# Down projection of the gated MLP: a part's first product one tile sooner, the third copy into SBUF, the next strip's sums later, one buffer apart for the summed pieces

## Chip, core and metric

One core of one Trainium2 chip runs the whole program in one launch. The metric is the time of an execution on the device in microseconds (us), as a median over runs. The profile is one further execution with the hardware profiler on.

## What is computed

Two residual layers on a 512 x 1024 activation (SEQ 512, D_MODEL 1024), each a token mixer and a gated MLP with d_ff = 2816. The mixers (gated linear attention in layer 0, softmax attention in layer 1) are not touched. The part that matters is the MLP:

```
def conv_ffn(h, w_up, w_conv, b_conv, w_down):
    u = h @ w_up
    u = lax.conv_general_dilated(
        u, w_conv[:, None, :], window_strides=(1,), padding=[(1, 1)],
        dimension_numbers=('NWC', 'WIO', 'NWC'), feature_group_count=u.shape[-1]) + b_conv
    val, gate = jnp.split(u, 2, axis=-1)
    return (jax.nn.silu(gate) * val) @ w_down
...
    for i in range(DEPTH):
...
        x = x + conv_ffn(rmsnorm(x, norm_ffn[i]), ffn_w_up[i], ffn_w_conv[i],
                         ffn_b_conv[i], ffn_w_down[i])
```

## The kernel before

**Numbers in two pieces.** Every float32 operand of a matmul is held as a high piece (fp32r) and a low piece, the rest. One product is then three matmuls: high by high, high by low, low by high.

**Tiles of the MLP.** The hidden width 2816 is 22 strips of 128 columns; strip m has a value half and a gate half. For each m, `act_up` (L656) makes two tiles of 128 x 512 in PSUM, t = 0 in a bank with the tag "acc" and t = 1 in a bank "s". Each takes 8 x 3 = 24 matmuls of 512 columns (L332 to L334). Behind them DVE scales (u, L672), ACT and DVE do the convolution (y: L674, L675, L676), ACT applies silu (L678), and DVE multiplies the two (L679). The activations of strips 2p and 2p+1 are then turned into the operands of the down product by `prepare` (L688): POOL and DVE form differences, and the helper `split` cuts each into two pieces on ACT (L685) and DVE (L686).

**Parts of the down product.** The first 16 strips are multiplied with the down weights by a scheme of Strassen's kind, in two parts of eight strips each, `down_part` (L712). By the table `DOWN_AFTER` = {9: 0, 17: 1}, part 0 stands behind strip m = 9 and part 1 behind m = 17, in both layers. A part has four strips n, and a strip has seven products of 12 matmuls each, 256 columns wide (all on L730; the tile that they write is called r). Their order in strip n: product 1 into r1 (`begin`), a copy r2 <- r1 on ACT (L739), product 6 onto r2, a copy r3 <- r2 (ACT, L747), 7 into r4, 2 onto r1, 5 onto r2, a third copy of r2 into the right half of r3's bank (ACT, L752), a DVE addition of r1 to x (L753), product 4 onto the left half of r3, product 1 of the next strip, two DVE subtractions of r4 and of the whole r3 from x (L758, L759), product 3 onto r2, and an addition of r2 to x (L761).

**Weights.** `Weights` loads a strip of 1 MB into one of two buffers "raw" (issued on SP, L129) and makes its pieces in the order of the list `todo`, some pieces ahead of their use. An up tile's piece is a copy on ACT (high, L190) and a subtraction on DVE (low, L191). A strip of the down weights has four pieces, h = 0 to 3 (`summed`, L144):

- h = 0 holds the operands of products 7 and 1: two sums on DVE (L150, L151, the second in place in raw), then high on ACT (L173) and low on DVE (L174).
- h = 1, for 5 and 6, is a sum on DVE (L155), then the same two lines.
- h = 2, for 2 and 4, has both copies on ACT (L169, L170); the low one is finished by an accumulating DMA that POOL issues (L180).
- h = 3, for 3, is half as wide (L162, L164, L165).

High pieces have tag "wh", low pieces "wl", four buffers each of 128 x 1024, shared by all weights.

**What orders the work.** The source is not the order on the engines: a scheduler in the compiler places each engine's instructions, and matmuls of one product can be set ahead of the rest of it. On each engine the result runs in order, and an instruction that waits holds up all behind it.

Of the kernel before, what the change touches and what calls it, by code (L numbers as in the profile page):

```python
# [8 lines left out]
F32 = mybir.dt.float32  # L9
F32R = mybir.dt.float32r  # L10
# [4 lines left out]
P = 128  # L15
S = 512
# [38 lines left out]
def hybrid_encoder_kernel(  # L55
# [39 lines left out]
    def pair(tag, bufs, dt, n):  # L95
        return sp.tile([P, 2 * S], dt, tag=tag, bufs=bufs, name=nm(n))
# [14 lines left out]
    class Weights:  # L111
# [2 lines left out]

        def __init__(self):
            self.todo, self.made, self.raw, self.by_dma, self.pending = [], {}, {}, [], []
            self.sums = {}

        def add(self, src, strips=None, pieces=2):
            for i in strips or range(src.shape[0]):  # L120
# [4 lines left out]
        def make(self, key):  # L125
            src, i, h = key
            if h == 0 and (id(src), i) not in self.raw:
                t = sp.tile([P, 4 * S], F32, tag="raw", bufs=2, name=nm("raw"))
                sync.dma_start(t, src[i])  # L129
                self.raw[id(src), i] = t  # L130
            if (id(src), i) in self.sums:
                self.made[id(src), i, h] = self.summed(self.raw[id(src), i], self.sums[id(src), i], h)
                return
            r = self.raw[id(src), i][:, h * 2 * S : (h + 1) * 2 * S]
            hi, lo = pair("wh", 4, F32R, "wh"), pair("wl", 4, F32R, "wl")
            if any(src is a and i < n for a, n in self.by_dma):
                act.activation(hi, r, AF.Copy)
                act.activation(lo, r, AF.Copy, scale=-1.0)  # L138
                self.pending.append((lo, r))
            else:  # L140
                self.split(hi, lo, r, 2 if src is w_vg and i < 2 else 1, src is w_vg and i == 0 and h == 0)
            self.made[id(src), i, h] = (hi, lo)

        def summed(self, raw, sums, h):  # L144


            a21, a11, a12, a22 = (raw[:, n * S : (n + 1) * S] for n in range(4))
            if h == 0:
                sums["e"] = e = big(F32, "sum")
                dve.tensor_tensor(e[:, :S], a21, a22, ALU.add)  # L150
                dve.tensor_tensor(a21, a21, a11, ALU.add)  # L151
                r = raw[:, : 2 * S]
            elif h == 1:
                e = sums["e"]
                dve.tensor_tensor(e[:, S:], e[:, :S], a11, ALU.add)  # L155
                r = e
            elif h == 2:
                r = raw[:, 2 * S :]
            else:
                e = sums["e"]  # L160
                r = tmp("sq", "sum4")
                dve.tensor_tensor(r, e[:, S:], a12, ALU.add)  # L162
                hi, lo = (sp.tile([P, S], F32R, tag="sq", bufs=3, name=nm(n)) for n in ("wh4", "wl4"))
                act.activation(hi, r, AF.Copy)  # L164
                dve.tensor_tensor(lo, r, hi.bitcast(F32), ALU.subtract)  # L165
                return hi, lo
            hi, lo = pair("wh", 4, F32R, "wh"), pair("wl", 4, F32R, "wl")
            if h == 2:
                act.activation(hi, r, AF.Copy)  # L169
                act.activation(lo, r, AF.Copy, scale=-1.0)  # L170
                self.pending.append((lo, r))
            else:
                act.activation(hi, r, AF.Copy)  # L173
                dve.tensor_tensor(lo, r, hi.bitcast(F32), ALU.subtract)  # L174
            return hi, lo
# [32 lines left out]

    W = Weights()
    up = [w_up[i] for i in range(2)]  # L210
    down = [w_down[i] for i in range(2)]

    def add_ffn(layer):
        first = 0
        for m, part in DOWN_AFTER.items():
            W.add(up[layer], range(first, m + 1))
            W.add(down[layer], range(part * NQ, (part + 1) * NQ), 4)
            first = m + 1
        W.add(up[layer], range(first, FC))
        W.add(down[layer], range(NPART * NQ, down[layer].shape[0]))  # L220

    for a in (w_vg, w_kq, w_gout):
        W.add(a)
# [185 lines left out]
    def gla(norm, nxt):  # L409
# [38 lines left out]

        rraw = sp.tile([P, KC * 32], F32, tag="sq", bufs=3, name="rraw")
        sync.dma_start(rraw, w_r)  # L450
        rw = pair("wh", 4, F32R, "rw")
# [198 lines left out]


    def ffn(layer, norm, cw, nxt):
        plain = {}
        quads = {}

        def act_up(m):  # L656

            res, pss = [], []
            for t in range(2):
                ps = bank("s" if t else "acc", "up")  # L660
                feature_tile(*W.half(up[layer], 2 * m + t, 3 if m in DOWN_AFTER and t else 1), norm.hl, ps)
                pss.append(ps)
                if m == 0 and t == 0:
                    norm.tokens()
                elif m == 0:
                    norm.rows()
            for t in range(2):
                ps = pss[t]
                cc = ((layer * 2 + t) * FC + m) * 4
                w = lambda i: cw[:, cc + i : cc + i + 1]  # L670
                u = tmp("u", "u")
                dve.tensor_tensor(u, ps, norm.R, ALU.mult)  # L672
                y = tmp("t", "y")
                act.activation(y, u, AF.Identity, scale=w(1), bias=w(3))  # L674
# [3 lines left out]
            act.activation(res[1], res[1], AF.Silu)  # L678
            dve.tensor_tensor(res[0], res[0], res[1], ALU.mult)  # L679
            return res[0]  # L680
# [28 lines left out]

        PLACE = {1: (0, S), 7: (0, 0), 6: (1, S), 5: (1, 0), 2: (2, 0), 4: (2, S), 3: (3, 0)}  # L710

        def down_part(part, then):  # L712

            src = down[layer]
            pairs = [quads.pop(part * NQ + i) for i in range(NQ)]
            st = [{} for _ in range(NQ)]
            pieces = {}

            def product(n, i, dst, start):
                h, o = PLACE[i]
                if (n, h) not in pieces:
                    pieces[n, h] = W.piece(src, part * NQ + n, h, 3)
                wh, wl = pieces[n, h]
                for j in range(NQ):
                    sl = slice(o + j * P, o + (j + 1) * P)
                    mh, ml = pairs[j][i]
                    for a, (w, m) in enumerate(((wh, mh), (wh, ml), (wl, mh))):
                        mm(dst, w[:, sl], m, start=start and j == 0 and a == 0, stop=j == NQ - 1 and a == 2,  # L730
                           skip_group_check=True)
                W.flush()

            def begin(n):
                r = st[n]
                r[1] = bank("acc", "r1")
                product(n, 1, r[1][:, :H], True)
                r[2] = bank("acc", "r2")
                act.activation(r[2][:, :H], r[1][:, :H], AF.Copy)  # L739

            begin(0)
            for n in range(NQ):
                r, c, d = st[n], x[2 * n], x[2 * n + 1]
                r1, r2 = r[1][:, :H], r[2][:, :H]
                product(n, 6, r2, False)
                r3 = bank("s", "r3")
                act.activation(r3[:, :H], r2, AF.Copy)  # L747
                r4 = bank("pt", "r4")
                product(n, 7, r4[:, :H], True)
                product(n, 2, r1, False)  # L750
                product(n, 5, r2, False)
                act.activation(r3[:, H:], r2, AF.Copy)  # L752
                dve.tensor_tensor(c[:, :H], c[:, :H], r1, ALU.add)  # L753
                product(n, 4, r3[:, :H], False)
# [3 lines left out]
                dve.tensor_tensor(two(d), two(d), two(r4[:, :H]).to_broadcast([P, 2, H]), ALU.subtract)  # L758
# [3 lines left out]
                if n == 1 and then is not None:  # L762
                    then()

        def end(c, ps):
            if nxt is not None or c < KC - 1:
# [10 lines left out]
        last = None  # L777
        for m in range(FC):
            y = act_up(m)
            if m >= 2 * NQ * NPART:  # L780
# [5 lines left out]
            elif m not in DOWN_AFTER:  # L786
                prepare(m // 2, last, y)
            if m in DOWN_AFTER:
                down_part(DOWN_AFTER[m], (lambda: prepare(m // 2, last, y)) if m < 2 * NQ * NPART else None)
        cur, open_ = None, {}  # L790
        for u, (c, k) in enumerate(PLAIN):
            if u % 8 == 0:
                cur = W.half(down[layer], NPART * NQ * 2 + u // 8)
# [313 lines left out]
```

## Time and profile before

| what | value |
|---|---|
| median of 3 runs | 1137.65 us (1137.04 to 1137.72) |
| the profiled execution, its own time | 1136.9 us |
| its span, from the first to the last instruction | 1135.2 us |
| PE (matmul) busy | 1119.9 us, 99% of the span |
| DVE, ACT, POOL busy | 793.1, 551.2, 121.4 us (70%, 49%, 11%) |
| matmuls of the down parts (L730), high and low | 164.5 and 125.5 us, 896 and 448 matmuls |
| PE waits put down to the copy on L739 | 5.7 us in 4 waits |

In the rows of the profile, L730 is a line of the kernel as it was before, an arrow reads "output <- inputs", and "[1.62 <-ACT r L739]" says that the engine was idle for 1.62 us ahead of this row and that the ACT instruction of L739 on tile r ended the wait. Matmuls overlap, so PE's busy time says less than the distance between the starts of two rows.

### The profile page before, as it was taken

To read this page: it belongs to the slowest core of one execution; us is meant where nothing else is said; L and a number is where in the kernel's file an instruction comes from. 1 tells how busy PE (TensorE), PEld (TensorE's weight loads), DVE (VectorE), ACT (ScalarE), POOL (GpSimd) and SP (SyncE) were. 2 spreads that over 40 slices of the span, in tenths; PEclk is the share of its full clock that TensorE was granted. 3 is DMA by queue.
4 is the path that set the end of the run, shared out by engine and by line. 5 is a ranking of instruction groups with operands and counts; after the bars stand their busy time and mean duration, and the time that the engine had idled before them with its cause. 6 is when DMAs were issued, how large, how long until landed. Compare 5 with 4: busy or idle time off the path is not lost.

```text
span 1135.2 us, 14636 instructions
## 1 busy us (share of the span) xinstructions
PE 1119.9 (99%) x5836; PEld 957.2 (84%) x5836; DVE 793.1 (70%) x1204; ACT 551.2 (49%) x818; POOL 121.4 (11%) x114
## 2 busy tenths in 40 slices
PE   9999999999999999999999999999999999999998
PEld 7788888888889988898888888888888998889887
DVE  6786653667888577776755679766788857777672
ACT  6565233444456444553464667544445644455340
POOL 0104110001011000000014333000100100000000
PEclk9999999999999999999999999999999999999999
DMA  6322210323225432253357633032322543225322
GB/s 234 144 97 89 75 46 29 111 75 111 74 75 133 164 111 96 73 133 146 130 125 173 157 103 75 1 112 74 111 75 75 132 165 112 89 79 132 147 74 75
DMA packets 22292, 120.16 MB, mean 106 GB/s; under 512 B 2640, under 2 KB 3280, under 8 KB 10704
## 3 DMA queue, kind: packets, MB, share of 16 engines
q1 hardware_dynamic: 17328, 102.29, 25.8%
q0 software_dynamic: 4608, 16.78, 7.8%
q8 instruction: 46, 0.75, 0.3%
q14 instruction: 22, 0.18, 0.0%
q10 hardware_dynamic: 288, 0.15, 0.0%
HBM read 100.34 MB, written 2.10 MB: 90 GB/s over the span
## 4 chain that ended last, share of the span: by engine, by line
PE 86%; DVE 6%; DMA 2%; issue 2%; ACT 2%; POOL 1%; SPq 0%; DVEq 0%; ACTq 0%; POOLq 0%
PE r L730 12%; PE up L333 12%; PE up L332 12%; PE up L334 11%; PE op L389 8%; PE vg L363 7%; PE dn L334 2%; PE dn L333 2%; PE dn L332 2%; PE o L614 2%; DMA wl<-raw 1%; PE pt L968 1%; PE av L363 1%; PE kv L590 1%; DMA raw<-in_w_down_dram 1%
## 5 line engine op out<-in xcount | busy, mean ns | idle before, releaser
L332 PE MATMUL up<-xhl,wh 128*128 128x512 f32 x704 | 274.3, 390 | 0.0
L333 PE MATMUL up<-xhl,wh 128*128 128x512 f32 x704 | 274.0, 389 | 0.0
L334 PE MATMUL up<-xhl,wl 128*128 128x512 f32 x704 | 273.9, 389 | 0.0
L190 ACT ACTIVATE wh<-raw 128x1024 fp32r<-128x1024 f32 x132 | 139.0, 1056 | 212.7 <-PE up L333 114.3
L191 DVE TENSOR_TENSOR wl<-raw,wh 128x1024 fp32r<-128x1024 f32 x132 | 163.8, 1241 | 52.4 <-ACT wh L190 52.4
L730 PE MATMUL r<-gu,wh 128*128 128x256 f32 x896 | 164.5, 285 | 7.1 <-ACT r L739 5.7
L332 PEld LDWEIGHTS up<-xhl,wh 128*128 128x128 f32 x704 | 132.2, 188 | 27.2
L333 PEld LDWEIGHTS up<-xhl,wh 128*128 128x128 f32 x704 | 132.2, 188 | 27.2
L334 PEld LDWEIGHTS up<-xhl,wl 128*128 128x128 f32 x704 | 132.1, 188 | 27.2
L730 PEld LDWEIGHTS r<-gu,wh 128*128 128x128 f32 x896 | 139.1, 191 | 11.8 <-ACT r L739 6.6
L730 PE MATMUL r<-gu,wl 128*128 128x256 f32 x448 | 125.5, 285 | 1.1 <-DVE wl L174 0.9
L672 DVE TENSOR_TENSOR u<-up,R 128x512 f32<-128x512 f32 x88 | 60.3, 687 | 45.0 <-PE up L334 45.0
L674 ACT ACTIVATE y<-u,cw 128x512 f32<-128x512 f32 x88 | 71.1, 811 | 35.5 <-DVE u L672 35.5
L730 PEld LDWEIGHTS r<-gu,wl 128*128 128x128 f32 x448 | 84.9, 191 | 2.3 <-DVE wl L174 1.3
L363 PE MATMUL vg<-wh,xhl 128*128 128x512 f32 x256 | 79.9, 391 | 0.3 <-DVE halfneg L250 0.3
L389 PE MATMUL op<-oT,wh 128*128 128x512 f32 x256 | 70.9, 395 | 0.0
L675 DVE SCALAR_TENSOR_TENSOR y<-u,cw,y 128x511 f32<-128x511 f32 x88 | 65.6, 747 | 4.2 <-ACT y L674 4.1
L676 DVE SCALAR_TENSOR_TENSOR y<-u,cw,y 128x511 f32<-128x511 f32 x88 | 65.8, 750 | 2.3
L678 ACT ACTIVATE y<-y 128x512 f32<-128x512 f32 x44 | 27.8, 632 | 71.8 <-DVE y L676 71.7
L180 POOL DMA_DIRECT2D wl<-raw x32 | 28.2, 881 | 303.6 <-ACT wl L138 140.4
L363 PEld LDWEIGHTS vg<-wh,xhl 128*128 128x128 f32 x256 | 47.9, 188 | 10.7 <-ACT sq L306 0.6
L389 PEld LDWEIGHTS op<-oT,wh 128*128 128x128 f32 x256 | 47.1, 188 | 9.7 <-ACT oT L629 0.3
(215 smaller groups left out, 1842.4 us busy)
## 6 DMA issues: line engine op xcount, KB each, us to landing
raw<-in_w_up_dram SPq DMA_DIRECT2D x44, 1024.0 KB, 4.8
raw<-in_w_down_dram SPq DMA_DIRECT2D x22, 1024.0 KB, 4.8
wl<-raw POOLq DMA_DIRECT2D x32, 512.0 KB, 4.6
raw<-in_w_vg_dram SPq DMA_DIRECT2D x6, 1024.0 KB, 4.8
raw<-in_w_akq_dram SPq DMA_DIRECT2D x5, 1024.0 KB, 4.8
raw<-in_w_kq_dram SPq DMA_DIRECT2D x4, 1024.0 KB, 4.8
raw<-in_w_gout_dram SPq DMA_DIRECT2D x4, 1024.0 KB, 4.8
raw<-in_w_aout_dram SPq DMA_DIRECT2D x4, 1024.0 KB, 4.8
```

What stands on the lines that cost most here:

```text
L190: act.activation(hi[:, sl], r[:, sl], AF.Copy)
L191: dve.tensor_tensor(lo[:, sl], r[:, sl], hi[:, sl].bitcast(F32), ALU.subtract)
L332: mm(ps, wh, mh, start=start, stop=False)
L333: mm(ps, wh, ml, start=False, stop=False)
L334: mm(ps, wl, mh, start=False, stop=stop)
L363: mm(ps[j][:, :width], hl[k][i == 2][:, j * P : (j + 1) * P], (wl if i == 1 else wh)[:, sl], start=k == 0 and i == 0, stop=k == KC - 1 and ...
L389: mm(pss[ng][n], wt[:, sl], mv, start=k == 0 and i == 0, stop=k == KC - 1 and i == 2)
L672: dve.tensor_tensor(u, ps, norm.R, ALU.mult)
L674: act.activation(y, u, AF.Identity, scale=w(1), bias=w(3))
L675: dve.scalar_tensor_tensor(y[:, 1:], u[:, : S - 1], w(0), y[:, 1:], ALU.mult, ALU.add)
L676: dve.scalar_tensor_tensor(y[:, : S - 1], u[:, 1:], w(2), y[:, : S - 1], ALU.mult, ALU.add)
L730: mm(dst, w[:, sl], m, start=start and j == 0 and a == 0, stop=j == NQ - 1 and a == 2, skip_group_check=True)
```

## The change

- **First product sooner.** `down_part` becomes a generator. For m = 9 and m = 17, `act_up` starts it between the two up tiles, so product 1 of strip 0 and the copy behind it are issued ahead of tile t = 1. The rest is run where the part stood. In `todo` the piece h = 0 of the part's first strip changes places with the piece of the up tile t = 1 of strip m. The call of `prepare` in the middle of the part takes its arguments from `late`.
- **Third copy.** It goes to an SBUF tile r5 of 128 x 256 (tag "u") and no longer to the right half of r3's bank. The subtraction of r3 (512 wide) becomes two of 256: one of r5, one of r3.
- **Sums later.** The two sums of h = 0 (L150, L151) are placed behind `self.last`, the low piece of h = 3 that was issued last, by `issue_after`.
- **Buffers.** "wh" and "wl" go from four buffers to three, and the pieces h = 1 get "sh" and "sl" with one buffer each. The space is the same.

```
+            self.sums, self.last = {}, None
...
-            hi, lo = pair("wh", 4, F32R, "wh"), pair("wl", 4, F32R, "wl")
+            hi, lo = pair("wh", 3, F32R, "wh"), pair("wl", 3, F32R, "wl")
...
-                dve.tensor_tensor(e[:, :S], a21, a22, ALU.add)
-                dve.tensor_tensor(a21, a21, a11, ALU.add)
+                with tc.issue_after(self.last.ins) if self.last else ExitStack():
+                    dve.tensor_tensor(e[:, :S], a21, a22, ALU.add)
+                    dve.tensor_tensor(a21, a21, a11, ALU.add)
...
-                dve.tensor_tensor(lo, r, hi.bitcast(F32), ALU.subtract)
+                self.last = dve.tensor_tensor(lo, r, hi.bitcast(F32), ALU.subtract)
...
-            hi, lo = pair("wh", 4, F32R, "wh"), pair("wl", 4, F32R, "wl")
+            if h == 1:
+                hi, lo = pair("sh", 1, F32R, "sh"), pair("sl", 1, F32R, "sl")
+            else:
+                hi, lo = pair("wh", 3, F32R, "wh"), pair("wl", 3, F32R, "wl")
...
+            at = len(W.todo) - 4 * NQ - 1
+            W.todo[at : at + 2] = W.todo[at + 1], W.todo[at]
...
+                if t == 0 and m in DOWN_AFTER:
+                    down.append(down_part(DOWN_AFTER[m], m))
+                    next(down[-1])
...
             begin(0)
+            yield
...
-                r3 = bank("s", "r3")
-                act.activation(r3[:, :H], r2, AF.Copy)
+                r3 = bank("s", "r3")[:, :H]
+                act.activation(r3, r2, AF.Copy)
...
-                act.activation(r3[:, H:], r2, AF.Copy)
+                r5 = tmp("u", "r5", H)
+                act.activation(r5, r2, AF.Copy)
...
-                dve.tensor_tensor(d, d, r3, ALU.subtract)
+                dve.tensor_tensor(d[:, H:], d[:, H:], r5, ALU.subtract)
+                dve.tensor_tensor(d[:, :H], d[:, :H], r3, ALU.subtract)
...
-                down_part(DOWN_AFTER[m], (lambda: prepare(m // 2, last, y)) if m < 2 * NQ * NPART else None)
+                late = last, y
+                for _ in down[-1]:
+                    pass
```

In the changed file the lines have moved: L741 is the product that was L730, L338 to L340 the matmuls of the up tiles, L750 the first copy, L194 an up piece's high copy, L177 the high copy of h = 0 and 1, L178 their low piece, L151, L152 and L156 the sums, L685 the y on ACT.

**PE, part 0 of layer 0.** The up tile of strip 9 with t = 0 ends; r is the accumulator of product 1, gu are its operands, wh and wl the weight pieces. Before, the first product stands behind the tile t = 1, and after it product 7 is begun and then product 6 (r_2688):

```order
L333 MATMUL up_2611<-xhl_1826,wh_2583 128x512
L334 MATMUL up_2611<-xhl_1826,wl_2584 128x512
L730 MATMUL r_2669<-gu_2001,wh_2617 128x256 x2
L730 MATMUL r_2669<-gu_2001,wl_2618 128x256
...
L730 MATMUL r_2669<-gu_2495,wl_2618 128x256
L730 MATMUL r_2713<-gu_2003,wh_2617 128x256 x2
L730 MATMUL r_2713<-gu_2003,wl_2618 128x256
L730 MATMUL r_2713<-gu_2168,wh_2617 128x256 x2
L730 MATMUL r_2688<-gu_2003,wh_2622 128x256 x2
```

With the change it stands ahead of the tile t = 1 (up_2645), and product 6 (r_2643) follows behind that tile:

```order
L339 MATMUL up_2582<-xhl_1826,wh_2540 128x512
L340 MATMUL up_2582<-xhl_1826,wl_2541 128x512
L741 MATMUL r_2616<-gu_2001,wh_2588 128x256 x2
L741 MATMUL r_2616<-gu_2001,wl_2589 128x256
...
L741 MATMUL r_2616<-gu_2495,wl_2589 128x256
L338 MATMUL up_2645<-xhl_1646,wh_2617 128x512
...
L340 MATMUL up_2645<-xhl_1826,wl_2618 128x512
L741 MATMUL r_2643<-gu_2003,sh_2622 128x256 x2
```

The 24 matmuls of an up tile now stand between product 1 and product 6.

**PE, part 1 of layer 0**, behind the up tile of strip 17 with t = 0. In this part the changed order is not a whole product and then a whole tile:

```order
L340 MATMUL up_3731<-xhl_1826,wl_3687 128x512
L741 MATMUL r_3765<-gu_2937,wh_3737 128x256 x2
L741 MATMUL r_3865<-gu_2939,wh_3737 128x256 x2
L338 MATMUL up_3794<-xhl_1646,wh_3766 128x512
L339 MATMUL up_3794<-xhl_1646,wh_3766 128x512
L741 MATMUL r_3765<-gu_2937,wl_3738 128x256
L741 MATMUL r_3765<-gu_3312,wh_3737 128x256 x2
...
L340 MATMUL up_3794<-xhl_1646,wl_3767 128x512
...
L741 MATMUL r_3792<-gu_2939,sh_3771 128x256 x2
```

Four matmuls of products 1 and 7 and two of the tile t = 1 stand first, then the rest of product 1, then the rest of the tile. Before, the first of these rows was followed at once by all 24 matmuls of the tile t = 1, and product 1 began behind them.

**ACT at the same place.** Before, from the last `split` ahead of the part:

```order
L685 ACTIVATE gu_3720<-y_3708 128x512
L173 ACTIVATE wh_3758<-raw_3753 128x1024
L173 ACTIVATE wh_3763<-sum_3755 128x1024
L169 ACTIVATE wh_3767<-raw_3753 128x1024
L170 ACTIVATE wl_3768<-raw_3753 128x1024
L674 ACTIVATE y_3798<-u_3796,cw 128x512
L164 ACTIVATE wh_3816<-sum_3814 128x512
L674 ACTIVATE y_3804<-u_3802,cw 128x512
L739 ACTIVATE r_3832<-r_3813 128x256
```

With the change:

```order
L696 ACTIVATE gu_3728<-y_3716 128x512
L177 ACTIVATE wh_3737<-raw_3732 128x1024
L194 ACTIVATE wh_3766<-raw_3684 128x1024
L177 ACTIVATE sh_3771<-sum_3734 128x1024
L173 ACTIVATE wh_3775<-raw_3732 128x1024
L174 ACTIVATE wl_3776<-raw_3732 128x1024
L750 ACTIVATE r_3792<-r_3765 128x256
```

The high piece of h = 0 is still the first instruction behind the `split`; the up tile's piece, which stood ahead of that `split`, is now second, and the copy r2 <- r1 has come forward past two y and the piece of h = 3. On DVE, the two sums of this piece (L150 and L151, now L151 and L152) still stand behind the multiplication that closes strip 16 (L679, now L690), with one `split` instruction between them.

More of the change, by code (lines that the diff above doesn't have):

```diff
@@ L210, in hybrid_encoder_kernel @@
     up = [w_up[i] for i in range(2)]
-    down = [w_down[i] for i in range(2)]
+    down_w = [w_down[i] for i in range(2)]
     def add_ffn(layer):
@@ L652, in ffn @@
     def ffn(layer, norm, cw, nxt):
+        w_dn = down_w[layer]
         plain = {}
+        down = []
         quads = {}
@@ L710, in ffn, with down_part @@
         PLACE = {1: (0, S), 7: (0, 0), 6: (1, S), 5: (1, 0), 2: (2, 0), 4: (2, S), 3: (3, 0)}
-        def down_part(part, then):
-            src = down[layer]
+        def down_part(part, m):
+            src = w_dn
             pairs = [quads.pop(part * NQ + i) for i in range(NQ)]
```

23 lines of the change are left out of this document (11 added, 12 removed).

## Prediction

> **What bounds the kernel now.** I read the page first, then PE's waits, then the starts on PE around each part. From the page: the span, PE's granted clock in 40 slices, and the group of the down products' matmuls.
>
> ```profile
> span 1135.2 us, 14636 instructions
> PEclk9999999999999999999999999999999999999999
> L730 PE MATMUL r<-gu,wh 128*128 128x256 f32 x896 | 164.5, 285 | 7.1 <-ACT r L739 5.7
> ```
>
> PE has the full clock throughout, and the idle time ahead of the down products is 7.1 us, 5.7 of it put down to the first copy. The table of PE's waits (engine, line, what it waited for: total, times, longest) shows what can be won:
>
> ```profile
> PE r L730 <- ACT r L739: 5.7, 4, 1.6
> PE z L483 <- DVE rst L472: 1.3, 1, 1.3
> ...
> PE r L730 <- ACT r L752: 1.0, 2, 0.5
> PE r L730 <- DVE wl L174: 0.9, 2, 0.6
> ...
> PE r L730 <- DMA wl<-raw: 0.2, 1, 0.2
> ```
>
> One wait of L739 stands in each of the four parts. PE is the bound; the others count only where PE stands still for them. So I measure each part by PE's starts. The rows are start, duration, engine, line and operation; they are the first matmul of the tile t = 1 and the first matmul behind the next strip's first tile, for the four parts in order of time.
>
> ```profile
> 335.25 0.39 PE L332 MATMUL up<-xhl,wh 128*128 128x512 f32 x1
> 388.96 0.39 PE L332 MATMUL up<-xhl,wh 128*128 128x512 f32 x1
> 465.12 0.39 PE L332 MATMUL up<-xhl,wh 128*128 128x512 f32 x1
> 521.20 0.39 PE L332 MATMUL up<-xhl,wh 128*128 128x512 f32 x1
> 874.65 0.39 PE L332 MATMUL up<-xhl,wh 128*128 128x512 f32 x1
> 928.56 0.39 PE L332 MATMUL up<-xhl,wh 128*128 128x512 f32 x1
> 1004.72 0.39 PE L332 MATMUL up<-xhl,wh 128*128 128x512 f32 x1
> 1060.38 0.39 PE L332 MATMUL up<-xhl,wh 128*128 128x512 f32 x1
> ```
>
> The stretches are 53.71, 56.08, 53.91 and 55.66 us. What they would be without a wait follows from these rows of part 1, layer 0 (end of the tile t = 1, product 1, and the wait):
>
> ```profile
> 470.56 0.40 PE L730 MATMUL r<-gu,wh 128*128 128x256 f32 x2
> ...
> 472.00 0.40 PE L730 MATMUL r<-gu,wh 128*128 128x256 f32 x2
> ...
> 472.36 0.40 PE L730 MATMUL r<-gu,wh 128*128 128x256 f32 x2
> 474.38 0.50 PE L730 MATMUL r<-gu,wh 128*128 128x256 f32 x2 [1.62 <-ACT r L739]
> ```
>
> A tile takes 470.56 - 465.12 = 5.44, a product 472.00 - 470.56 = 1.44. Two tiles and 28 products make 10.88 + 40.32 = 51.20. **So the parts lose 2.51, 4.88, 2.71 and 4.46, together 14.6 us**: the most that this change can win there. A wait costs more than its idle time: two matmuls after 472.36 PE should go on at 472.60, and went on at 474.38.
>
> **Part 0 of both layers (a gain).** Here the first copy is late because ACT runs a y ahead of it that itself waits for DVE. ACT, DVE and PE in layer 0:
>
> ```profile
> 331.92 1.06 ACT L173 ACTIVATE wh<-raw 128x1024 fp32r<-128x1024 f32 x1 [1.70 <-DVE raw L151]
> ...
> 342.99 0.81 ACT L674 ACTIVATE y<-u,cw 128x512 f32<-128x512 f32 x1 [1.27 <-DVE u L672]
> 343.71 0.36 ACT L739 ACTIVATE r<-r 128x256 f32<-128x256 f32 x1
> ```
> ```profile
> 333.02 1.22 DVE L174 TENSOR_TENSOR wl<-raw,wh 128x1024 fp32r<-128x1024 f32 x1
> ```
> ```profile
> 344.13 0.50 PE L730 MATMUL r<-gu,wh 128*128 128x256 f32 x2 [1.25 <-ACT r L739]
> ```
>
> With the change product 1 wants to begin at 335.25. Its low piece is done at 333.02 + 1.22 = 334.24, so nothing waits. Product 1 ends 1.44 later, and the tile's 5.44 us cover a copy of 0.36 and the delay in front of it. I leave 0.4 for short waits: -2.1 in layer 0, -2.3 in layer 1, **together -4.4**.
>
> **Part 1 of both layers (a loss).** Here the pieces come too late for the new place. ACT, then DVE, layer 0:
>
> ```profile
> 466.18 0.63 ACT L685 ACTIVATE gu<-y 128x512 fp32r<-128x512 f32 x1 [0.76 <-DVE y L679]
> 468.22 1.06 ACT L173 ACTIVATE wh<-raw 128x1024 fp32r<-128x1024 f32 x1 [1.41 <-DVE raw L151]
> 469.19 1.05 ACT L173 ACTIVATE wh<-sum 128x1024 fp32r<-128x1024 f32 x1
> ...
> 473.96 0.36 ACT L739 ACTIVATE r<-r 128x256 f32<-128x256 f32 x1
> ```
> ```profile
> 465.45 0.69 DVE L679 TENSOR_TENSOR y<-y,y 128x512 f32<-128x512 f32 x1 [0.76 <-ACT y L678]
> 466.06 0.69 DVE L150 TENSOR_TENSOR sum<-raw 128x512 f32<-128x512 f32 x1
> ...
> 469.32 1.23 DVE L174 TENSOR_TENSOR wl<-raw,wh 128x1024 fp32r<-128x1024 f32 x1
> ```
>
> The high piece waits for the sum L151, and the sums stand on DVE behind the multiplication that closes strip 16. The orders show these rows where they were, so the piece is done at 468.22 + 1.06 = 469.28 as before. PE, which had the tile t = 1 to run until 470.56, now has product 1 first, at 465.12, and behind it the four matmuls that need the same piece. **It stands still for 469.28 - 465.12 = 4.16, with 0.1 to start again 4.3.** Two matmuls of product 1 and two of product 7 take 0.48. Then the tile's high piece, second on ACT, is done at 469.19 + 1.05 = 470.24, not at 469.76: 0.6 more with the restart. Product 1 goes on at about 470.8; its low piece is done at 469.32 + 1.23 = 470.55, and the tile's low piece, next on DVE, at about 471.7, when product 1 ends. The copy, now fifth behind 468.22 at 0.95 each, is done before 473.4; product 6 comes near 476.9, so L739 does not count. Up to here the part loses 4.3 + 0.6 = 4.9 where it lost 474.38 - 472.60 = 1.78 and 0.1 to start again, 1.88. In layer 1 the same piece comes later by the same measure:
>
> ```profile
> 1007.82 1.06 ACT L173 ACTIVATE wh<-raw 128x1024 fp32r<-128x1024 f32 x1 [1.41 <-DVE raw L151]
> ```
>
> 1008.88 - 1004.72 = 4.16 again.
>
> **Third copy and sums of the next strip.** The rows of strips 0 and 1, DVE, POOL, PE:
>
> ```profile
> 478.76 0.41 DVE L753 TENSOR_TENSOR x<-x,r 128x256 f32<-128x256 f32 x1
> ...
> 482.13 0.69 DVE L150 TENSOR_TENSOR sum<-raw 128x512 f32<-128x512 f32 x1 [1.15 <-DMA raw<-in_w_down_dram]
> ```
> ```profile
> 484.61 0.86 POOL L180 DMA_DIRECT2D wl<-raw  x1 [11.31 <-ACT wl L170]
> ```
> ```profile
> 484.01 0.39 PE L730 MATMUL r<-gu,wl 128*128 128x256 f32 x1 [0.56 <-DVE wl L174]
> 489.59 0.39 PE L730 MATMUL r<-gu,wl 128*128 128x256 f32 x1 [0.16 <-DMA wl<-raw]
> ```
>
> With r5 in SBUF, product 4 no longer waits for a copy in its bank: L752's two waits go, 0.5 each in part 1, and 0.26 around each (1.88 less 1.62 above): -0.8 each. Writing to SBUF isn't shown for this copy; the accumulators' copies take 0.36 and the additions of 256 columns 0.41, so 0.36 to 0.41, and nothing waits for r5 but DVE. The split subtraction adds 16 DVE instructions: between nothing and 0.41 each, beside PE as long as the piece behind them isn't late.
>
> In strip 1 it is late. The sums stand behind the x addition of L753's kind, the two subtractions behind product 4's end, and only then comes the low piece. DVE is rid of the row that waited 1.15 for raw in front of it, but everything stands 2.5 later, from product 6 on. I work the low piece out as 1.3 to 1.6 late where it was 0.56 (with restarts 0.82): +0.7. The high and low copies of h = 2 stay behind on ACT, the low one done near 487.2 to 488; the DMA then takes 489.59 - 484.61 = 4.98, so it lands at 492.5 to 493.1, against PE there at 491.3 to 491.6: 0.9 to 1.8, I take 1.2 against 0.42, so +0.8. Bounds for both: from -1.2 (they are hidden) to +2.5. Strips 2 and 3 lost 1.0 before and I leave that.
>
> Part 1, layer 0: 4.9 - 1.88 - 0.8 + 0.7 + 0.8 = **+3.7**; half of strips 2's and 3's short waits go where the sums no longer block DVE, -0.5: +3.2. In layer 1 I take the same, +3.2. Together +6.4, bounds +1 to +9.
>
> **Buffers.** Three instead of four for high and low pieces: between two pieces of an up tile lie 5.44, and the copy and the subtraction take 1.06 and 1.23; nothing waits. The one "sh" is free after product 5, and products 4, 1 and 3 (4.3) lie before its next use, against 2.3 to make it. Zero, up to +0.7 a strip if this is wrong.
>
> **Early in layer 0.** The order on DVE changes too at the wait of L483:
>
> ```profile
> 37.41 0.64 ACT L471 ACTIVATE rst<-rf 128x512 fp32r<-128x512 f32 x1 [4.17 <-DVE rf L469]
> ```
> ```profile
> 38.54 0.68 DVE L472 TENSOR_TENSOR rst<-rf,rst 32x512 fp32r<-32x512 f32 x1
> ```
>
> A piece's subtraction of 1.22 stood between, and L472 is now ahead of it: it can begin at 37.41 + 0.64 = 38.05 and no longer 38.54, **-0.45**.
>
> **Sum.** -4.4 + 6.4 - 0.45 = +1.55 us on the profiled 1136.9 (span 1135.2 and 1.7 around it). The median of before is 0.75 above that execution; +1.55 on 1137.65 is **1139.2**.
>
> **Rivals.**
>
> A, faster: only the first wait of part 1 is lost. If strips 1 to 3 hide their pieces as part 0's do, part 1 loses 4.9 in all, as it did before (4.88 and 4.46, so +0.5), and the total is -4.4 + 0.5 - 0.45 = -4.4: 1133.3. For it speaks that L150's wait for raw is out of the way; against it that the whole chain on ACT is shifted and the h = 2 DMA had no slack (0.16).
>
> B, slower: the idle stretch slows PE itself. No stretch between 5 and 1130 us was idle beyond 1.62 us, and the clock was full in all 40 slices, so the trace says nothing of 4.2. If PE went on at half its pace for half a tile to a whole one, it would lose 2.7 to 5.4 in a part; once in the run that is 1142 to 1144.6. It decides only if the stop is as long as I say. [...]
>
> C, slower: the single "sh" or the third buffer holds up each strip. 16 strips at 0.7 are +11: 1148 to 1150. The margins above speak against it.
>
> D: the moves do nothing for PE, as when the scheduler had kept the old order: 1137.65. The orders show otherwise.
>
> **Chances and range.** Forecast 0.48 (1137 to 1142), A 0.20, B 0.20, C 0.07, D 0.05. A measurement of this kernel can tell 0.2%, 2.3 us, so "same" reaches from 1135.4 to 1139.9. The forecast's own range lies 0.28 in it and 0.20 above it. Faster: 0.20; same: 0.28 + 0.05 = 0.33; slower: 0.20 + 0.20 + 0.07 = 0.47. The range for 8 in 10 reaches from most of A to the upper end of B: 1132.5 to 1145.5; it leaves out the lower part of A and C.
>
> **What would show it.** Right: no wait of PE for the first copy; in part 0 stretches of 51.5 to 51.8; in part 1 a wait of about 4.2 us on L741 for the high piece L177, twice, and stretches near 59. Wrong: a wait at part 1 below 3 (the pieces were made sooner than the order says), waits at the wh pieces of up tiles (C), or starts 0.45 apart where 0.23 is usual (B).

## The result and the profile after

The changed kernel takes 1139.27 us (median of 20 runs, 1137.52 to 1141.36), the kernel before 1137.68 us (20 runs, 1136.58 to 1141.43). The ratio is 1.0013, with a 95% interval of 1.0006 to 1.002: slower by a tenth of a per cent, inside the 0.2% that was called no change. The profiled execution took 1138.57 us, its span is 1136.4.

From the page of the changed kernel, the rows that answer to those of before:

```profile
span 1136.4 us, 14630 instructions
PEclk9999999999999999899999999999999999999999
L741 PE MATMUL r<-gu,wh 128*128 128x256 f32 x640 | 119.6, 287 | 8.3 <-ACT wh L177 8.1
```

The wait for the first copy is gone from the group of the down products, and a larger one for a high piece has come. The clock row has an 8 in it where all slices were 9. (The group has fewer matmuls because those with h = 1 read "sh" and "sl" and form groups of their own.) The table of PE's waits has nothing of L750, L765 or L478 any more. The first of these two lines is new, and the DMA's has grown from 0.2 to 2.5:

```profile
PE r L741 <- ACT wh L177: 8.1, 2, 4.0
PE r L741 <- DMA wl<-raw: 2.5, 2, 1.6
```

PE's starts around the four parts. A part now runs from the first matmul behind the tile t = 0 of strip 9 or 17 to the first matmul of the tile t = 1 of the next strip, which is the same work as before.

```profile
334.17 0.40 PE L741 MATMUL r<-gu,wh 128*128 128x256 f32 x2
...
385.23 0.39 PE L338 MATMUL up<-xhl,wh 128*128 128x512 f32 x1
...
461.16 0.39 PE L340 MATMUL up<-xhl,wl 128*128 128x512 f32 x1
465.59 1.22 PE L741 MATMUL r<-gu,wh 128*128 128x256 f32 x4 [4.04 <-ACT wh L177]
...
521.77 0.39 PE L338 MATMUL up<-xhl,wh 128*128 128x512 f32 x1
...
875.22 0.40 PE L741 MATMUL r<-gu,wh 128*128 128x256 f32 x2
...
926.47 0.39 PE L338 MATMUL up<-xhl,wh 128*128 128x512 f32 x1
...
1002.40 0.39 PE L340 MATMUL up<-xhl,wl 128*128 128x512 f32 x1
1006.83 0.57 PE L741 MATMUL r<-gu,wh 128*128 128x256 f32 x1 [4.04 <-ACT wh L177]
...
1061.88 0.39 PE L338 MATMUL up<-xhl,wh 128*128 128x512 f32 x1
```

Part 0 takes 385.23 - 334.17 = 51.06 us in layer 0 and 926.47 - 875.22 = 51.25 in layer 1. In part 1 the tile t = 0 ends at 461.16 + 0.23 = 461.39 (0.23 is the usual distance of two starts), the part takes 60.38; in layer 1 it runs from 1002.63 and takes 59.25. The same sum for every kernel of this study, in us (part 0 and part 1 of layer 0, then of layer 1; medians in their own series, against the kernel before in that series):

| kernel | part 0 | part 1 | part 0 | part 1 | median us | ratio to before, 95% |
|---|---|---|---|---|---|---|
| before | 53.7 | 56.1 | 53.9 | 55.7 | 1137.68 | |
| changed | 51.1 | 60.4 | 51.3 | 59.3 | 1139.27 | 1.0013 (1.0006 to 1.002) |
| move in part 0 alone | 51.1 | 54.5 | 51.4 | 54.6 | 1128.57 | 0.9915 (0.9901 to 0.993) |
| without the move | 52.1 | 54.6 | 52.1 | 54.6 | 1129.75 | 0.9922 (0.9909 to 0.9935) |
| the move alone | 54.3 | 60.2 | 52.9 | 60.0 | 1144.32 | 1.0048 (1.0035 to 1.0061) |
| stop filled | 51.1 | 58.1 | 51.1 | 58.4 | 1134.78 | 0.9973 (0.996 to 0.9985) |
| sooner piece | 51.1 | 55.4 | 51.1 | 52.9 | 1126.36 | 0.9892 (0.9879 to 0.9906) |
| sooner piece, old buffers | 53.5 | 53.8 | 52.4 | 55.0 | 1131.02 | 0.9939 (0.9927 to 0.9951) |
| sooner piece, old sums | 52.2 | 55.7 | 54.4 | 52.8 | 1127.82 | 0.9906 (0.9891 to 0.9922) |
| sooner piece, old third copy | 52.7 | 57.1 | 52.7 | 54.0 | 1132.21 | 0.9945 (0.9933 to 0.9958) |
| sooner piece, h = 2 first | 51.1 | 53.2 | 51.1 | 54.6 | 1126.20 | 0.9892 (0.9879 to 0.9906) |
| sooner piece, four ahead | 51.1 | 51.1 | 51.1 | 51.1 | 1120.67 | 0.9851 (0.9835 to 0.9866) |
| the same, five ahead, h = 2 first | 51.1 | 51.4 | 51.1 | 51.6 | 1121.24 | 0.9848 (0.9834 to 0.9863) |
| four ahead, without the move | 52.1 | 55.4 | 52.1 | 58.1 | 1133.20 | 0.9963 (0.995 to 0.9977) |

No part of any kernel is shorter than 51.06, which is called the floor from here on. So the change brings part 0 to the floor in layer 0 and near it in layer 1, and lengthens part 1 by 4.3 and 3.6. Why part 1 stops is in the rows of ACT and then of DVE in the changed kernel:

```profile
462.44 0.63 ACT L696 ACTIVATE gu<-y 128x512 fp32r<-128x512 f32 x1 [0.76 <-DVE y L690]
464.48 1.06 ACT L177 ACTIVATE wh<-raw 128x1024 fp32r<-128x1024 f32 x1 [1.41 <-DVE raw L152]
```
```profile
461.72 0.69 DVE L690 TENSOR_TENSOR y<-y,y 128x512 f32<-128x512 f32 x1 [0.76 <-ACT y L689]
462.32 0.69 DVE L151 TENSOR_TENSOR sum<-raw 128x512 f32<-128x512 f32 x1
...
463.71 0.69 DVE L152 TENSOR_TENSOR raw<-raw 128x512 f32<-128x512 f32 x1
```

The piece is done at 464.48 + 1.06 = 465.54 and PE starts at 465.59. What PE does behind that is in the view by stages (length, PE busy with its number of matmuls, then PE's clock, DMA):

```profile
461.00:463.00 2.00, 0.55 (x3) 1.00 0.00 0
463.00:465.00 2.00, 0.00 (x0) 0.79 0.00 0
465.00:467.00 2.00, 1.41 (x5) 0.50 0.01 4
467.00:469.00 2.00, 2.00 (x9) 0.50 0.22 29
...
471.00:473.00 2.00, 2.00 (x10) 1.00 0.97 295
```

PE was busy all the while from 467 to 471, at a granted clock of 0.50 until nearly 471. Busy time doesn't show the slower pace, the starts do: matmuls of 512 columns begin at 469.69, 470.12 and 470.55, so 0.43 apart, where 0.23 is usual. All 20 timed runs of the changed kernel have a mean granted clock of 0.993 to 0.997, so none escaped it.

### The profile page after: what moved, and what is told of

Read it like the earlier page. It is cut to its first block, busy times and chain, and to the rows that moved or that the text cites. A ratio compares the mean times of both kernels' runs of the same rounds, so it can differ in the third digit from the quotient of the medians.

```text
span 1136.4 us, 14630 instructions
## 1 busy us (share of the span) xinstructions
PE 1119.8 (99%) x5836; PEld 960.1 (84%) x5836; DVE 795.5 (70%) x1220; ACT 551.6 (49%) x818; POOL 120.2 (11%) x114
## 4 chain that ended last, share of the span: by engine, by line
PE 92%; DVE 3%; issue 2%; DMA 1%; ACT 1%; POOL 0%; SPq 0%; DVEq 0%; POOLq 0%; ACTq 0%
PE up L338 13%; PE up L339 13%; PE up L340 13%; PE r L741 12%; PE vg L369 8%; PE op L395 8%; PE dn L339 2%; PE dn L340 2%; PE dn L338 2%; PE o L620 2%; PE pt L984 1%; DMA wl<-raw 1%; PE av L369 1%; PE kv L596 1%; PE A L338 1%
## 5 line engine op out<-in xcount | busy, mean ns | idle before, releaser
L338 PE MATMUL up<-xhl,wh 128*128 128x512 f32 x704 | 275.3, 391 | 0.0
L340 PE MATMUL up<-xhl,wl 128*128 128x512 f32 x704 | 274.2, 390 | 0.0
L194 ACT ACTIVATE wh<-raw 128x1024 fp32r<-128x1024 f32 x132 | 139.5, 1057 | 228.0 <-PE up L339 108.2
L340 PEld LDWEIGHTS up<-xhl,wl 128*128 128x128 f32 x704 | 132.4, 188 | 27.6
L338 PEld LDWEIGHTS up<-xhl,wh 128*128 128x128 f32 x704 | 132.5, 188 | 27.2
L741 PE MATMUL r<-gu,wh 128*128 128x256 f32 x640 | 119.6, 287 | 8.3 <-ACT wh L177 8.1
L741 PEld LDWEIGHTS r<-gu,wh 128*128 128x128 f32 x640 | 101.5, 195 | 10.0 <-ACT wh L177 9.6
L741 PE MATMUL r<-gu,wl 128*128 128x256 f32 x320 | 91.5, 287 | 2.6 <-DMA wl<-raw 2.5
L685 ACT ACTIVATE y<-u,cw 128x512 f32<-128x512 f32 x88 | 71.2, 811 | 42.9 <-DVE u L683 42.9
L741 PEld LDWEIGHTS r<-gu,wl 128*128 128x128 f32 x320 | 61.9, 194 | 3.8 <-DMA wl<-raw 3.2
```

Source lines behind the costliest of these rows:

```text
L194: act.activation(hi[:, sl], r[:, sl], AF.Copy)
L338: mm(ps, wh, mh, start=start, stop=False)
L340: mm(ps, wl, mh, start=False, stop=stop)
```

## The experiments

**The move in part 0 alone.** Part 1 begins its first product behind the tile t = 1 again.

```
+            if part == 0:
+                at = len(W.todo) - 4 * NQ - 1
+                W.todo[at : at + 2] = W.todo[at + 1], W.todo[at]
...
+                    if m == 9:
                         next(down[-1])
```

> The change, but in part 1 the first product stays behind the tile t = 1 and the order of the pieces there is the old one. Theory W (part 1 loses because its first product asks for a piece that is not made; part 0 and the early wait gain): part 0 gives 2 x 2.7, the early wait 1.1, part 1 stands within 1 us of before in each layer; no half clock anywhere; 1130 to 1132 us. Rival (the loss in part 1 comes from the later sums and the fewer buffers, not from the first product): part 1 stays 3 to 4 us longer than before in each layer, 1138 to 1140 us.

1128.57 us: W, and 1.4 us below its range. There is no stop, and part 1 is shorter than before by 1.6 and 1.1, a little more than W allowed. What it waits for is this:

```profile
PE r L743 <- DMA wl<-raw: 3.0, 4, 1.0
PE r L743 <- ACT r L752: 2.3, 2, 1.1
```

L752 here is the first copy, late in part 1 as it was before. It follows that the loss of the changed kernel comes from the move in part 1 and not from its other edits.

**The sooner piece.** One more piece is made ahead at the tile t = 1 of strips 8 and 16, the move stays in both parts.

```
-... 3 if m in DOWN_AFTER and t else 1)
+... 3 if m in DOWN_AFTER and t else 2 if m + 1 in DOWN_AFTER and t else 1)
```

> The change with one more piece made ahead at the tile t = 1 of strips 8 and 16, so that the first down piece of a part is issued one strip sooner; the first product stays moved in both parts. Theory W: no stop of 4 us ahead of the first product of part 1, no half clock, part 1 shorter than before by 2 to 4 us in each layer; 1125 to 1129 us. Rival (DVE and ACT are full there, so the sooner piece only makes the y of strip 16 or the next pieces late, and a stop of 2 us or more comes back elsewhere in part 1): 1131 to 1136 us.

1126.36 us: W in the time, and the stop ahead of product 1 is gone in both layers. In layer 0 a sign of the rival came as well: a stop of 2.1 us stands in strip 1 of part 1, for the accumulating DMA, with a stage at half clock behind it, which W had ruled out. That part is 4.3 above the floor and only 0.7 shorter than before (2.8 in layer 1).

```profile
PE r L741 <- DMA wl<-raw: 3.0, 2, 2.1
```
```profile
485.00:487.00 2.00, 2.00 (x14) 0.82 0.61 70
487.00:489.00 2.00, 2.00 (x12) 0.50 0.84 287
```

POOL issued this DMA 18.1 us behind the tile t = 0 in both layers. PE went on 5.66 us after the issue in layer 0 and 4.54 in layer 1, so about 1.1 of the 2.1 us is a slower DMA and not a later one. Two of the four timed runs have a mean granted clock of 1.000 and are at least 1.0 us faster than the two with 0.998, so the half clock doesn't come every time here.

**The stop filled.** 16 matmuls of 512 columns, whose results are overwritten, stand ahead of product 1 of part 1.

```
                 r[1] = bank("acc", "r1")
+                if n == 0 and part == 1:
+                    for i in range(16):
+                        mm(r[1], norm.hl[i % KC][0][:, :P], norm.hl[i % KC][0], start=True, stop=True)
```

> The change with 16 matmuls of 512 columns (3.6 us of work that is thrown away, into the accumulator of product 1 ahead of it) in the stop of part 1, in both layers. Theory C (the stop has two prices: the wait of 4.2 us, and PE at half pace behind it): the clock stays full, product 1 begins at the same time as without them, part 1 is shorter than in the changed kernel by 1.8 us in layer 0 and 1.1 in layer 1; 1136 to 1137 us. Rival (the half pace costs nothing, since the pieces behind would have held PE up as long): the clock is full and the time stays at 1138.8 to 1139.6 us. If the filling itself costs: over 1140 us.

1134.78 us: C, 1.2 us below its range. PE's rows in layer 0, and then the stage in which the clock was half before:

```profile
463.35 3.79 PE L750 MATMUL r<-xhl 128*128 128x512 f32 x16
467.56 0.50 PE L741 MATMUL r<-gu,wh 128*128 128x256 f32 x2 [0.42 <-ACT wh L177]
468.82 0.39 PE L741 MATMUL r<-gu,wl 128*128 128x256 f32 x1 [0.76 <-DVE wl L178]
```
```profile
466.00:468.00 2.00, 1.58 (x8) 1.00 0.00 0
```

Product 1 begins 467.56 - 463.35 = 4.21 behind the tile, as in the changed kernel (465.59 - 461.39 = 4.20), so the filling costs nothing and the piece is as late. The clock stays at 1.00, and the parts are shorter by 2.3 and 0.9. That is the gain in all. At the 84th matmul of the part's products, a strip's number, the changed kernel is 1.5 and 0.6 us behind this one, counted from the tile t = 0: the price of the half pace by itself, after the wait for the low piece (0.76), which the half pace had hidden. The rest, 0.8 and 0.3, is in later waits of strips 1 and 2 (in layer 0 the DMA wait is 1.55 in the changed kernel and 0.95 here, in strip 1 of layer 1 it is 0.94 and 1.22); whether those follow from the half pace isn't separated. The medians, of different series, differ by 4.5 us and the four parts by 3.4; where the remaining 1 us lies is not known.

**The move alone**, on the kernel before: no SBUF copy, no later sums, old buffers.

> The kernel before with the first product sooner in both parts (and the two pieces changed over), without the SBUF copy, the later sums and the buffers apart. Theory W: part 0 gains 2.1 to 2.7 us in each layer, part 1 has the stop of 4.2 us and the half clock as in the changed kernel, and besides the two short waits for the third copy; the early wait of 1.3 us is back: 1139.5 to 1141.5 us. Rival (the stop comes from the other edits): no stop, 1130 to 1133 us.

1144.32 us, 3 us above the range. The stop is there, as W says, but part 0 does not gain what W says: it is 0.5 longer than before in layer 0 (54.3) and 1.0 shorter in layer 1 (52.9).

```profile
PE r L737 <- ACT wh L173: 7.2, 2, 3.6
PE r L737 <- DMA wl<-raw: 3.8, 4, 1.6
```

1.6 of the DMA waits stand in part 0 of layer 0 (strip 2). So the move needs the other edits to gain its 2.7 even in part 0. The next three kernels take them away one at a time, with the sooner piece, so that no stop lies over it.

**Old buffers** (four "wh" and "wl", none apart):

> The kernel with the sooner piece, with the buffers of before (four high and four low, none apart). Theory Z (buffers cost and bring nothing in the parts, and the early wait of L483 hangs on them): the wait for L472 of about 1.3 us is back, the parts stay within 0.5 us each: 1.0 to 1.6 us more than with the sooner piece alone. Rival (the buffer apart is what lets the pieces of a strip be made in time, as seen where only the first product was moved, with a wait of 1.8 us for the h = 2 piece in part 0): 3 to 6 us more.

1131.02 us, 4.7 more: the rival, though Z's early wait is back too. Both parts 0 lose (2.4 and 1.3), and part 1 of layer 1 loses 2.1. Part 1 of layer 0 is 1.6 shorter: its DMA wait is 0.9 here, and no half clock follows it (the execution's mean granted clock is 1.000).

```profile
PE r L738 <- DMA wl<-raw: 5.9, 6, 1.5
PE z L486 <- DVE rst L475: 1.2, 1, 1.2
```

**Old sums** (no `issue_after`):

> The kernel with the sooner piece, with the sums of the next strip where they were. Theory S (the later sums are what makes the h = 2 piece of strip 1 in part 1 land late): that wait of 1.1 to 2.2 us is under 0.5 in both layers, and 1 to 4 us less in all. Rival (the later sums are needed, since a sum that waits for its raw strip on DVE holds up the low pieces behind it): waits for low pieces or for the DMA of 0.5 us and more in several strips, 1 to 4 us more in all.

1127.82 us, 1.5 more. The 95% intervals of the two ratios overlap, so this difference isn't clear of noise, and the profiled execution was the slowest of four, 1130.94 against 1127.01 to 1128.01, so its lengths in the table overstate it. S has fallen: the DMA of strip 1 is late all the same (2.4). What comes is a wait that neither theory named, for the first copy (L749 here) of strip 1 in part 0, 3.1 us of it in layer 1. It is hardly as long in the three faster runs:

```profile
PE r L740 <- ACT r L749: 3.9, 2, 3.1
PE r L740 <- DMA wl<-raw: 3.3, 2, 2.4
```

**Old third copy** (in r3's bank, one subtraction of 512):

> The kernel with the sooner piece, with the third copy in r3's bank and one subtraction of 512. Theory K (the copy holds up product 4 where ACT is late): waits of 0.5 us for the third copy in part 1, 0.8 us with the restart in each layer, 1 to 2 us more in all. Rival (ACT is early now, so nothing waits): within 0.5 us of the kernel with the sooner piece.

1132.21 us, 5.9 more, three times the most that K said. The mechanism is K's, the copy (L764 here) holds up PE; but it does so in all four parts, though the waits of before named it in two:

```profile
PE r L741 <- ACT r L764: 2.3, 4, 0.6
```

**The piece h = 2 first** in strips 1 to 3:

```
+            for n in range(1, NQ):
+                k = len(W.todo) - 4 * (NQ - n)
+                W.todo[k : k + 3] = W.todo[k + 2], W.todo[k], W.todo[k + 1]
```

A strip is then loaded ahead of whichever of its pieces comes first, no longer ahead of h = 0 alone.

> The kernel with the sooner piece, and for the strips 1 to 3 of each part the piece h = 2, which needs no sum, is made first of the four. Theory D (what is left in part 1 is the accumulating DMA that lands late, 1.1 us in one layer and 2.2 us and a stage at half clock in the other): the wait is gone, part 1 near 95 us in both layers from strip 17 to the last up tile, 2 to 4 us less in all. Rival (two copies on ACT ahead of the other pieces, and a third high buffer held longer, make product 1 of the next strip late by as much): within 1 us of the kernel with the sooner piece, or more.

1126.20 us, no change: the rival. The DMA waits are gone, and the pieces of strip 1's product 1 are late instead, by 0.7 and 0.8 us in each layer. In layer 1 the clock fell to half behind these two waits (0.54 from 1013 to 1015 and 0.61 from 1015 to 1017, which makes 3.4 us at 0.50), in layer 0 it did not: the execution's mean of 0.998 has room for one such stretch and not for two.

```profile
PE r L744 <- DVE wl L178: 1.7, 2, 0.8
PE r L744 <- ACT wh L177: 1.4, 2, 0.7
```

So ACT's order only passes the lateness on; all of strip 1's pieces are late together.

**Without the move**, the three other edits kept:

> The change without its first edit: third copy into SBUF, later sums and the buffers apart, but product 1 stays behind the tile t = 1 in both parts. Theory M (the sooner product takes the wait for the first copy away, and the other three keep new waits from taking its place): part 0 still loses 1.2 to 1.7 us per layer on the first copy, part 1 as in the kernel that moves part 0 alone, the early wait is gone; 1131 to 1134 us. Rival (the three others alone bring part 0 to its floor of 127.2 us from strip 9 to strip 17): no wait for the first copy in part 0, 1128 to 1130 us.

1129.75 us. In mechanism M, in size the rival: each part still waits for the first copy (L747 here), and yet part 0 is 1.6 and 1.8 shorter than before.

```profile
PE r L738 <- ACT r L747: 4.0, 4, 1.1
```

Of the part 0 of before, 0.9 us can be read from PE's starts. Its third copy (L752) held up PE there as well, each time too briefly for the table of waits:

```profile
350.47 0.89 PE L730 MATMUL r<-gu,wh 128*128 128x256 f32 x4
```

Two such matmuls take 0.40 and each further one 0.12, so four take 0.64 when nothing holds them; here it was 0.89, and 0.95 at the same place of strips 1 and 2. That is 0.25 + 0.31 + 0.31 = 0.87, in layer 1 about the same. The edit that removes it, the copy into SBUF, wasn't tried alone on the kernel before.

**Four pieces ahead** at the tile t = 1 of strips 9 and 17, with the sooner piece and the move:

```
-... 3 if m in DOWN_AFTER and t else 1)
+... 4 if m in DOWN_AFTER and t else 2 if m + 1 in DOWN_AFTER and t else 1)
```

> The kernel with the sooner piece, and at the tile t = 1 of strips 9 and 17 four pieces made ahead instead of three, so that the sums of strip 1 of the part stand on DVE ahead of the y of strip 9 or 17. Theory E (what is left in part 1 is that strip 1's pieces are late by 1 to 2 us, on DVE): its waits for the high piece and the DMA go, part 1 at 95 to 96 us in both layers, 1123 to 1125 us. Rival (the y that is pushed back holds up the copies on ACT, or a high buffer isn't free): a wait of 1 us or more comes back, 1126 us or more.

1120.67 us: E, 2.3 us below its range. The sums of strip 1 now stand on DVE ahead of the y of strips 9 and 17. Their first row in part 1 of layer 0, with the sooner piece and then here:

```profile
473.17 0.68 DVE L151 TENSOR_TENSOR sum<-raw 128x512 f32<-128x512 f32 x1
```
```profile
467.01 0.69 DVE L151 TENSOR_TENSOR sum<-raw 128x512 f32<-128x512 f32 x1
```

That is 12.0 and 5.9 us behind the tile t = 0. All four parts are at 51.06, and PE's table of waits holds nothing of the MLP:

```profile
PE warm L254 <- DVE bd L260: 1.3, 1, 1.3
PE vg L369 <- DVE halfneg L256: 0.3, 1, 0.3
PE s L338 <- ACT p L966: 0.3, 1, 0.3
```

This is the fastest kernel of the study, 1.5% below the kernel before (1.3 to 1.7%). **Five ahead with h = 2 first** goes the same way and isn't better:

> The same with five pieces ahead and the piece h = 2 first in strips 1 to 3. Theory E: neither the DMA nor the sums are late, part 1 near 95 us in both layers and part 0 at 127.2, no stage at half clock, 1122.5 to 1124.5 us. Rival (three high buffers are then all held, so the high piece of product 1 waits for product 7 or for the up tile to end): waits for high pieces in strip 1 of 1 us and more, 1126 us or more.

1121.24 us: E again, 1.3 us below its range. What the table of waits has left is one first copy that comes 0.3 us late.

**Four ahead without the move:**

> The kernel without the first product's move, with four pieces made ahead at the tile t = 1 of strips 9 and 17: it says what the move itself is worth once the pieces of strip 1 are in time. Theory M2 (the move is worth the wait for the first copy, 1.0 to 1.3 us with restart in each of the four parts, and nothing else): those four waits stay, the DMA waits of strip 1 go, 4 to 5.5 us more than the kernel with both sooner pieces, 1124.5 to 1126.5 us. Rival (the pieces made ahead are the whole gain, and the first copy is hidden behind them): within 1 us of that kernel, 1120 to 1122 us.

1133.20 us: both theories missed. The four waits for the first copy are there (0.8 at most), as M2 says, but the DMA waits did not go:

```profile
PE r L738 <- DMA wl<-raw: 5.4, 3, 2.7
PE r L738 <- ACT r L747: 3.0, 4, 0.8
```

The one of 2.7 us stands in strip 0 of layer 1, with half clock behind it (0.50 from 1012 to 1018), and one of 1.9 in strip 1 of layer 0. Both DMAs were issued as long after the tile as in the kernel with three ahead and no move, but PE went on 6.39 and 5.86 us after the issue, where that kernel has 4.78 and 4.54. So these DMAs were slower and not later; why, and whether in every run, isn't known. What can be said of the edit: without the move and the sooner piece, the sums of strip 1 come no earlier on DVE for being made ahead in the program (12.3 us behind the tile, 12.2 with three ahead). How much of the best kernel's gain belongs to the move alone therefore stays open; only the move in part 0 with three ahead is separated (1.1 and 0.7 us, from the kernel without the move to the one with it in part 0 alone).

## Why the prediction came out right

The place, the cause and the length of the stop were right. That the time is within 0.1 us of the forecast is luck: part 0 and the early wait gained more than was said, and a half clock that was not in the sum took it back. By its own steps:

- **Part 0, -4.4.** Measured -2.65 and -2.66, together -5.3. The floor was 51.06 and not 51.20, and no short wait remained in layer 0, where I left 0.4 in each. The cause was placed too narrowly. The sum gave all of it to the sooner product, but without the move part 0 has already lost 1.6 and 1.8 of its length, and with the move alone it gains 1.0 in one layer and loses 0.5 in the other. The third copy, which the sum counted in part 1 alone, cost some 0.9 in each part 0 as well.
- **The stop in part 1, 4.16 and 4.3 with the restart.** Right: 4.04 idle, 4.20 from end to start, the same in both layers, ended by the piece that was named. The move in part 0 alone and the sooner piece both remove it.
- **0.6 for the tile's high piece.** Not seen: L194, behind L177 on ACT, made that piece from 465.44 to 466.48, and PE, at half pace (granted clock 0.50), came to the tile at 466.61.
- **The clock.** The forecast had none of it, rival B all of it, and B came on top of the forecast, in every run. B's half pace, its 2.7 to 5.4 us in one part and its chance of 0.20 were my estimate, and no run shows that loss. In its place the granted clock fell to 0.50 in both layers, and the filled stop prices it at 1.5 us in layer 0 (6.8 us at half clock) and 0.6 in layer 1 (3.4 us), and at 2.3 and 0.9 with the later waits. B's trigger was a stop as long as mine, and that held; so did its sign, starts 0.43 apart. In layer 0 the clock of 0.79 between 463 and 465 puts the fall at 464.15, within the stop, 2.60 us behind PE's last matmul (until 461.55). In layer 1 PE was idle from 1002.79 to 1006.83, and the fall is at 1006.87, 4.08 us behind the last matmul. What sets the fall and the length of the half clock isn't shown by these two.
- **Strip 1 of part 1, +0.7 and +0.8.** The low piece cost nothing more than before (0.7 in all in layer 0, where 0.82 was lost before), the DMA cost 1.8 in layer 0, more than the 1.2 that I took, and 1.2 in layer 1, as I took it. POOL and PE in layer 0, as the rows of before:

```profile
486.45 0.86 POOL L184 DMA_DIRECT2D wl<-raw  x1 [15.95 <-ACT wl L174]
```
```profile
491.61 0.39 PE L741 MATMUL r<-gu,wl 128*128 128x256 f32 x1 [1.55 <-DMA wl<-raw]
```

  The DMA took 491.61 - 486.45 = 5.16, near the 4.98 used. The cause that I named, the later sums, isn't it: with the old sums the wait stays. That four pieces ahead remove it shows that strip 1's pieces as a whole stood too late.
- **Part 1 in sum, +3.2 in each layer.** Measured +4.3 and +3.6. The half pace with what followed it (+2.3, +0.9) and the DMA of layer 0 are the excess; the 0.6 and the waits of strips 2 and 3, which are gone in layer 0, are what was counted too much.
- **Buffers, zero.** Wrong in sign. The buffers apart bring 4.7 us where the piece is sooner, some 1.2 of it the early wait. What they bring in the changed kernel itself wasn't tried. The margins that I worked out say only that they do no harm.
- **Early in layer 0, -0.45.** The whole wait of 1.3 went, and the run with the old buffers has it back (1.2), so it hangs on the buffers. The subtraction that I named is only the smaller part: an instruction ahead of it on DVE, the CAST that makes smask, took 2.36 us before (L445) and takes 0.22 now (L451). It is long in the three kernels with the old buffers (1.76 to 2.36) and 0.21 or 0.22 in the other eleven; why the buffers make it long isn't shown.

The parts together were forecast at +2.0 and measured at +2.6, the early wait took back the rest. Rival A, that strips 1 to 3 hide their pieces, was wrong for this kernel; with four pieces ahead they do.

## What to carry to other kernels

Before a product is moved to an earlier place, look up when its operands are made, on the engine that makes them: a wait taken away at one end comes back in front of the product if the producer stays where it is. Then move the producer by the same distance: here two numbers of a look-ahead turned a change of +0.1% into -1.5%. And where several edits each remove one wait on the same path, take them away from the best kernel one at a time; alone on the kernel before, the main one showed a loss of half a per cent.

## What the runs showed of the hardware

**Half clock after a stop.** PE's granted clock fell to 0.50 in or behind the stops of 4.0 us (both layers of the changed kernel: from 464.15 to 470.98, which is 6.83 us, and from 1006.87 to 1010.28, 3.41 us) and behind one of 2.1 us (the kernel with the sooner piece, layer 0, shown above: the two stages of 0.82 around the one of 0.50 make 3.4 us). It did not fall after the waits of 1.6 us in the kernel before (1.00 from 472 to 476 and from 1012 to 1016). Length alone doesn't decide: in the kernel with the old sums a stop of 3.1 us went by at full clock.

```profile
888.00:891.00 3.00, 0.00 (x0) 1.00 0.63 205
891.00:894.00 3.00, 2.94 (x24) 1.00 0.36 150
```

With h = 2 first, shorter waits, of 0.7 and 0.8 us, were followed by half clock in layer 1 and not in layer 0. What decides isn't shown: none of this was varied by itself. A stop of 4.0 us thus cost more than its length here: filling it with matmuls that are thrown away kept the clock at 1.00 (462 to 472, layer 0) and gave 2.3 and 0.9 us back.

**The start of the program varies.** The same first matmuls at two paces, in the kernel with the move in part 0 alone and in the one with the filled stop; the instructions up to here are the same in both:

```profile
5.62 1.17 PE L370 MATMUL vg<-wh,xhl 128*128 128x512 f32 x4 [0.72 <-DVE halfneg L257]
37.96 0.40 PE L490 MATMUL z<-rst,gst 128*128 128x512 f32 x1
```
```profile
6.03 2.05 PE L369 MATMUL vg<-wh,xhl 128*128 128x512 f32 x4 [0.99 <-DVE halfneg L256]
40.41 0.40 PE L489 MATMUL z<-rst,gst 128*128 128x512 f32 x1
```

Four matmuls took 1.17 or 2.05 us (the next one began 1.00 and 1.85 us behind their first, so 0.25 and 0.46 a matmul), and the matmul z stood at 37.96 or 40.41. 2.4 us of difference between two single executions can come from there alone, more than this change is worth. The lengths of the parts do not have it, which is why the comparisons above go by them.
